# A hybrid decoder layer on one core: three rules and seven DMA issuers changed in a kernel that plans its own instruction order

## The chip, the cores and the metric

The kernel runs on one core of one Trainium2 chip. TensorE (PE), VectorE (DVE), ScalarE (ACT), GpSimd (POOL) and SyncE (SP) each work through their own queue in order; they meet through semaphores, and transfers run beside them. The metric is the device time of one launch in microseconds: the median of three runs before the change is 491.67 us (490.88 to 494.11).

## The reference

One layer on x of 256 tokens by 1024 channels, in float32. A conditioning vector c gives nine vectors of shift, scale and gate. Three sub-layers follow, each normalised first and added to the stream through its gate:

```python
mod = silu(c) @ w_ada + b_ada                       # 1024 x 9216, split in nine
n = modulate(rmsnorm(h, g_ffn1), sh1, sc1)
h = h + 0.5 * gt1 * swiglu(n, w1_gate, w1_up, w1_down)        # 1024 -> 2816 -> 1024
n = modulate(rmsnorm(h, g_mix), sh2, sc2)
h = h + gt2 * hybrid_mixer(n, w_in, w_pool, pool_scale, w_out)
n = modulate(rmsnorm(h, g_ffn2), sh3, sc3)
h = h + 0.5 * gt3 * swiglu(n, w2_gate, w2_up, w2_down)
return rmsnorm(h, g_final)
```

The mixer makes u, q, k, v with one projection. Four groups of 128 channels of u go through trailing means over 2, 4, 8 and 16 tokens (minus the token itself), a 128x128 map and a per-channel scale. Eight heads of 64 do causal attention with distance penalties over three sets of strided keys. Both halves are concatenated and projected by w_out.

## The kernel before

**Tiling and number format.** The 256 tokens are two tiles of 128 (t = 0 and 1). Every large product keeps float32 accuracy by three passes: an operand is split into a rounded copy `hi` and the remainder `lo`, and PE adds hi*hi, lo*hi and hi*lo in PSUM (`gemm`, lines 628 to 630; the same in lines 669, 699 and 1010). Weights come in 1 MB pieces named `raw` (SP issues them, line 515). ACT casts half a piece to `hi` (line 531), DVE subtracts to get `lo` (line 532). The conditioning product runs on DVE alone: line 520 reduces a piece of w_ada against silu(c) into columns of `mod`.

**Stages.** First feed-forward (PE tiles `ld`, `gu`, down projection into `accf`), then the mixer (`zp` gives u, q, k, v as `z`; `sc` scores, `p` probabilities, `pt` their transposes, `pts` the copies of those, `yt` the head outputs; `po` the pooled means, `pl` their copy, `pw` the map), then w_out into `accm`, then the second feed-forward (`le`, `gu`, `accf`). Between stages `norm_rows` (lines 565 to 585) works per token tile: the gate row tile `gt` times the accumulator, add to `h`, sum of squares half on ACT (line 575) and half on DVE (line 578), one addition (line 576) and one power (line 581) on GpSimd, scaled rows `xsb` or `xsc`, which PE transposes into `xtb` or `xtc` (line 558).

**The mixer's outputs.** They are split as well: `y[t]` is a pair of tiles, `nhy` (rounded) and `nly` (remainder), one pair for each token tile. Heads: `split` in lines 550 and 551, called from `heads_out` for t = 0, then t = 1, both out of the one PSUM tile `yt`. Pool groups: lines 959 and 960, for t = 0, then t = 1, out of the one PSUM tile `pw`.

**Gate rows.** `gate_rows` turns eight columns of `mod` into a row on all partitions: PE transposes (`gp`, line 617), ACT copies to `gs` (line 619), a transfer writes it to HBM (`gd`, line 621), and another, which waits for that, reads it back to 128 partitions (`gt`, line 623). It is called three times, for the gates of the three sub-layers.

**Mixer constants.** `bias` (two halves, lines 898 and 965), `band_all` (line 966), `wp_all` (line 967) and the final gain `gfb` (line 1042) are loads of 256 to 544 KB. In this kernel ACT issues all of these and the gate rows.

**The order.** `settle` records all instructions and `arrange` plans them five times over with a table of costs (`Item.cost`); the best of the five becomes the order of ACT, DVE and POOL and of PE, and is enforced. Three numbers of the plan matter here. A transfer is taken to have landed `LATE` ns after its modelled end. For PSUM tiles an instruction is put after the latest earlier user of the same tile on the same engine. Among ready instructions the one that is due first goes, looking `SOON` ns ahead. None of these costs is a measurement of this text; they only decide who stands behind whom.

Of the kernel before, what the change touches and what calls it, by code (L numbers as in the profile page):

```python
# [10 lines left out]
F32 = mybir.dt.float32  # L11
F32R = mybir.dt.float32r
AF = mybir.ActivationFunctionType
ALU = mybir.AluOpType

P = 128
S = 256
NT = S // P
D = 1024
# [159 lines left out]
STAGES = ("_ffn1_", "_mix_", "_ffn2_")  # L179
LANES = 8  # L180
SOON = 1400
LATE = 1000
PASSES = 5


# [88 lines left out]
def arrange(items, tiles, before):  # L274

    num = range(len(items))
    preds, history, uses, latest = [], {}, {}, {}
    for n in num:
        x, found = items[n], set(before.get(n, ()))
        for mine, accesses in ((False, x.reads), (True, x.writes)):  # L280
            for name, rows, mask in accesses:
                for k, wrote, r, m in history.get(name, ()):
                    if (wrote or mine) and r & rows and m & mask:
                        found.add(k)
        for mine, accesses in ((False, x.reads), (True, x.writes)):
            for name, rows, mask in accesses:
                kept = history.setdefault(name, [])
                if mine:
                    kept[:] = [e for e in kept if e[2] | rows != rows or e[3] | mask != mask]
                kept.append((n, mine, rows, mask))  # L290
                if n not in uses.setdefault(name, []):
                    uses[name].append(n)
                found.add(uses[name][0])
                if "_psp_" in tiles[name].tag or "_accp_" in tiles[name].tag:
                    found.add(latest.get((name, x.eng), n))
                    latest[name, x.eng] = n
        found.discard(n)
        preds.append(sorted(found))
    succs = [[] for _ in num]
# [15 lines left out]
    for _ in range(PASSES):  # L315
# [25 lines left out]
        while sum(map(len, order.values())) < len(items):  # L341
            pick = None
            for e in SIGNAL:
# [5 lines left out]
                if e == "PE":  # L349
                    n = min((n for n in at if at[n] <= t0 + 40), key=lambda n: items[n].prio)  # L350
                else:
                    now = sorted((n for n in at if at[n] <= t0 + 20), key=lambda n: due[n])
                    n = now[0]
                    if expect:
# [10 lines left out]
                        if h and u in at and near[u] + items[u].taken - due[n] - shift < h - 50:  # L365
                            n = u
# [80 lines left out]
def block_kernel(ctx, tc, w, vec, x, c, gf, wpool, bandd, biasd, out):  # L447
# [101 lines left out]
    def split(hi_ap, lo_ap, src):  # L549
        nc.scalar.copy(hi_ap, src)  # L550
        nc.vector.tensor_tensor(lo_ap, src, hi_ap.bitcast(F32), ALU.subtract)  # L551
# [61 lines left out]
    def gate_rows(gtm, factor):  # L613

        assert all(gtm * KD + j in done_mod for j in range(KD))
        pt = psp.tile([KD, P], F32, name=f"gp{gtm}", tag="ps")
        nc.tensor.transpose(pt, mod[:, ts(gtm, KD)], ident)
        sb = work.tile([KD, P], F32, name=f"gs{gtm}", tag="gs", bufs=1)
        nc.scalar.activation(sb, pt, AF.Copy, scale=factor)
        d = dram.tile([KD, P], F32, name=f"gd{gtm}", tag=f"gd{gtm}")  # L620
        nc.scalar.dma_start(d, sb)
        g = work.tile([P, D], F32, name=f"gt{gtm}", tag="gt", bufs=1)
        nc.scalar.dma_start(g, d.rearrange("(o a) b -> o (a b)", o=1).to_broadcast([P, D]))
        return g


# [268 lines left out]
    bias = [xp.tile([P, 4 * S], F32, name="bias0")]  # L895
    band_all = xp.tile([P, 4, 2 * P + 16], F32, name="band_all")
    wp_all = xp.tile([P, 4 * P], F32, name="wp_all")
    nc.scalar.dma_start(bias[0], biasd[:, 0:4 * S])

    def scores(hp):  # L900

# [24 lines left out]
    def heads_out(hp, v, y):  # L926
        pts = []
        for hd in (2 * hp, 2 * hp + 1):
            pt = psp.tile([P, 3, P], F32, name=f"pt{hd}", tag="ps")
            for i in range(3):  # L930
                nc.tensor.transpose(pt[:, i, :], probs[hd][:, ts(i, P)], ident)
            sb = xp.tile([P, 384], F32, name=f"pts{hd}", tag="pts", bufs=2)
            with urgent():
                nc.scalar.copy(sb, pt.rearrange("p a b -> p (a b)"))
            pts.append(sb)
        ps = psp.tile([P, S], F32, name=f"yt{hp}", tag="ps")
        for t, cs, qs in ((0, slice(0, S), slice(0, S)), (1, slice(P, S), slice(S, 384))):
            for e in range(2):
                mm(ps[e * DH:e * DH + DH, cs], v[t][:, ts(2 * hp + e, DH)], pts[e][:, qs], start=t == 0, stop=t == 1)
        with urgent():  # L940
            for t in range(NT):
                split(y[t][0][:, 4 + hp, :], y[t][1][:, 4 + hp, :], ps[:, ts(t, P)])

    def pool_group(g, u, y):
        bands, wp = band_all[:, g], wp_all[:, ts(g, P)]
# [9 lines left out]
        with urgent():  # L955
            sc = vecs[:, PS + g:PS + g + 1]
            for t in range(NT):
                yh, yl = y[t]
                nc.scalar.activation(yh[:, g, :], p2[:, ts(t, P)], AF.Copy, scale=sc)
                nc.vector.scalar_tensor_tensor(yl[:, g, :], p2[:, ts(t, P)], sc, yh[:, g, :].bitcast(F32),  # L960
                                               ALU.mult, ALU.subtract)

    after = finish1(1)
    bias.append(work.tile([P, 4 * S], F32, name="bias1", tag="gt", bufs=1))
    nc.scalar.dma_start(bias[1], biasd[:, 4 * S:8 * S])
    nc.scalar.dma_start(band_all, bandd)
    nc.scalar.dma_start(wp_all, wpool)
    QS = -DH ** -0.5
    y = [new_n(f"y{t}") for t in range(NT)]
    z = {}  # L970
# [68 lines left out]
        lead_step(1, j, n3, (2, 3, 0, 1), lead)  # L1039

    gfb = fp[0].tile([P, D], F32, name="gfb")
    nc.scalar.dma_start(gfb, gf.to_broadcast([P, D]))
    nc.scalar.mul(gfb, gfb, float(D) ** 0.5)

    def finish3(t):
# [69 lines left out]
```

## Time and profile before

| | |
|---|---|
| Median of three runs | 491.67 us (490.88 to 494.11) |
| The profiled execution | 492.43 us, span 490.7 us, mean granted PE clock 0.992 |
| PE busy | 474.2 us (97% of the span) |
| DVE, ACT, POOL busy | 358.2, 263.8, 10.8 us |
| Moved by transfers | 126.06 MB, 257 GB/s on average |

All times of the trace are microseconds from the start of the span. In a timeline row stand start, duration, engine, source line, operation, output<-inputs, shape, how many instructions were merged, and in brackets how long the engine had been idle and what ended that. A row of waits gives who waited for whom: total us, number of times, the longest. PE and ACT are pipelined, so instructions of one engine can overlap in a timeline; steps are then best read from start to start. ACTq is ACT's instruction issue: a transfer that it issues shows there.

### The profile page before, as it was taken

Reading aid. Unit: us, or ns where it says so; the run is one execution under the profiler, and the core shown is the slowest. Engines: PE = TensorE matmul, PEld = TensorE weight load, DVE = VectorE, ACT = ScalarE, POOL = GpSimd, SP = SyncE. Lnnn points to the kernel's source line nnn. Section 1 sums busy time; section 2 is a strip of 40 time slices with the busy share of each in tenths; the row PEclk is TensorE's granted clock in tenths of the full one; section 3 lists DMA queues with packets and bytes.
Section 4 is the critical chain, followed back from the end, with each engine's and each line's share of the span. In section 5 each row is a group of like instructions: output and inputs, shape, how many; then the busy total and the mean of one; then the engine's idle time right before and its main releaser. Section 6 shows DMA issues by size and latency. Waiting matters only on the chain.

```text
span 490.7 us, 6019 instructions
## 1 busy us (share of the span) xinstructions
PE 474.2 (97%) x2176; PEld 383.1 (78%) x2176; DVE 358.2 (73%) x579; ACT 263.8 (54%) x451; POOL 10.8 (2%) x22
## 2 busy tenths in 40 slices
PE   8999999999999999999997999999999999999993
PEld 5688888888888887777775777888888888888882
DVE  4989999987976856888996788755656765655243
ACT  3776676255444444896773486846543543544121
POOL 1000000000000001100000011000000000000000
PEclk9999999999999999999999999999999999999998
DMA  8999995998878882889758687475367758540002
GB/s 304 396 400 359 377 373 201 393 373 342 347 282 313 284 330 75 326 309 372 260 214 317 226 286 255 170 289 217 119 240 261 279 194 321 188 155 28 17 1 86
DMA packets 19232, 126.06 MB, mean 257 GB/s; under 512 B 2281, under 2 KB 3073, under 8 KB 4866
## 3 DMA queue, kind: packets, MB, share of 16 engines
q1 hardware_dynamic: 17568, 121.25, 65.1%
q10 hardware_dynamic: 1634, 4.43, 2.5%
q8 instruction: 17, 0.28, 0.2%
q14 instruction: 13, 0.11, 0.1%
HBM read 124.61 MB, written 1.06 MB: 256 GB/s over the span
## 4 chain that ended last, share of the span: by engine, by line
PE 81%; DVE 5%; DMA 4%; ACT 4%; issue 3%; POOL 2%; ACTq 0%; POOLq 0%; DVEq 0%
PE accf L669 20%; PE gu L628 9%; PE gu L630 9%; PE gu L629 9%; PE ld L699 8%; PE le L699 8%; PE accm L1010 3%; DMA raw<-in_w_dram 3%; PE zp L628 2%; PE zp L630 2%; PE zp L629 2%; PE ht L655 2%; ACT hi L531 1%; DVE lo L532 1%; DMA gd<-gs 1%
## 5 line engine op out<-in xcount | busy, mean ns | idle before, releaser
L532 DVE TENSOR_TENSOR lo<-raw,hi 128x1024 fp32r<-128x1024 f32 (+1 forms) x156 | 184.5, 1208 | 43.2 <-ACT hi L531 34.3
L531 ACT CAST hi<-raw 128x1024 fp32r<-128x1024 f32 (+1 forms) x156 | 159.5, 1043 | 91.8 <-DMA raw<-in_w_dram 34.4
L520 DVE CUSTOM_DVE_ANT_0 raw<-raw,cb,vecs 128x1024 f32<-128x1024 f32 x70 | 88.6, 1280 | 14.7 <-DMA raw<-in_w_dram 14.7
L669 PE MATMUL accf<-hi,hh 128*128 128x512 f32 x176 | 56.6, 395 | 0.2
L669 PE MATMUL accf<-hi,hl 128*128 128x512 f32 x176 | 55.6, 390 | 0.0
L669 PE MATMUL accf<-lo,hh 128*128 128x512 f32 x176 | 55.4, 390 | 0.0
L628 PE MATMUL gu<-hi,nhc 128*128 128x512 f32 x112 | 44.3, 395 | 0.0
L630 PE MATMUL gu<-lo,nhc 128*128 128x512 f32 x112 | 43.7, 390 | 0.0
L629 PE MATMUL gu<-hi,nlc 128*128 128x512 f32 x112 | 43.6, 389 | 0.0
L669 PEld LDWEIGHTS accf<-lo,hh 128*128 128x128 f32 x176 | 33.0, 188 | 7.0
L669 PEld LDWEIGHTS accf<-hi,hl 128*128 128x128 f32 x176 | 32.8, 188 | 7.1 <-DVE hl L551 0.5
L669 PEld LDWEIGHTS accf<-hi,hh 128*128 128x128 f32 x176 | 32.5, 188 | 7.3 <-ACT hh L550 1.1
L646 ACT ACTIVATE sg<-gu 128x256 f32<-128x256 f32 x24 | 9.1, 379 | 48.0 <-PE gu L630 48.0
L628 PE MATMUL gu<-hi,nha 128*128 128x512 f32 x80 | 31.7, 396 | 0.0
L630 PE MATMUL gu<-lo,nha 128*128 128x512 f32 x80 | 31.2, 390 | 0.0
L629 PE MATMUL gu<-hi,nla 128*128 128x512 f32 x80 | 31.1, 389 | 0.0
L649 DVE TENSOR_TENSOR pr<-sg,gu 128x256 f32<-128x256 f32 x24 | 10.0, 417 | 26.3 <-ACT sg L646 26.3
L551 DVE TENSOR_TENSOR hl<-ht,hh 128x256 fp32r<-128x256 f32 x44 | 16.4, 418 | 13.4 <-ACT hh L550 13.4
L628 PE MATMUL zp<-hi,nhb 128*128 128x512 f32 x64 | 26.2, 409 | 0.0
L550 ACT CAST hh<-ht 128x256 fp32r<-128x256 f32 x44 | 14.1, 379 | 22.3 <-PE ht L655 22.3
L630 PE MATMUL zp<-lo,nhb 128*128 128x512 f32 x64 | 25.2, 394 | 0.0
L629 PE MATMUL zp<-hi,nlb 128*128 128x512 f32 x64 | 25.2, 393 | 0.0
(171 smaller groups left out, 718.7 us busy)
## 6 DMA issues: line engine op xcount, KB each, us to landing
raw<-in_w_dram SPq DMA_DIRECT2D x112, 1024.0 KB, 5.7
raw<-in_w_dram SPq DMA_DIRECT2D x4, 512.0 KB, 7.9
gt<-gd ACTq DMA_DIRECT2D x3, 512.0 KB, 3.7
h<-in_x_dram SPq DMA_DIRECT2D x2, 512.0 KB, 5.4
bias<-in_bias_dram ACTq DMA_DIRECT2D x2, 512.0 KB, 3.9
out_dram<-o SPq DMA_DIRECT2D x4, 160.0 KB, 2.2
band_all<-in_band_dram ACTq DMA_DIRECT2D x1, 544.0 KB
gfb<-in_gf_dram ACTq DMA_DIRECT2D x1, 512.0 KB, 3.4
```

Source lines behind the costliest of these rows:

```text
L520: nc.vector.tensor_tensor_reduce(r, r, cb, 1.0, vecs[:, m:m + 1], ALU.mult, ALU.add, mod[:, m:m + 1])
L531: nc.scalar.copy(hi[:, o:o + n], src)
L532: nc.vector.tensor_tensor(lo[:, o:o + n], src, hi[:, o:o + n].bitcast(F32), ALU.subtract)
L550: nc.scalar.copy(hi_ap, src)
L551: nc.vector.tensor_tensor(lo_ap, src, hi_ap.bitcast(F32), ALU.subtract)
L628: mm(ps, nh[:, k, :], whi, start=first, stop=False)
L629: mm(ps, nl[:, k, :], whi, start=False, stop=False)
L630: mm(ps, nh[:, k, :], wlo, start=False, stop=last)
L649: nc.vector.tensor_tensor(pr, sg, ps[:, 256:512], ALU.mult)
L669: mm(accs[b], a[:, k, :], cols(ww, 2 * k + b), start=st, stop=sp)
L699: mm(banks[ci][t], n[t][a][:, j, :], cols(ww, lead_set(f, j).index(ci)), start=j == 0 and p == 0, stop=last and p == 2)
L1010: mm(acc2[t][b], a[:, k, :], cols(ww, 2 * kk + b), start=st, stop=sp)
```

## The change

Seven things change, in three groups.

The plan: `LATE` goes from 1000 to 2600, and the rule for PSUM tiles loses the engine, so that an instruction stands after the latest earlier user of the same tile on any engine ("turns" of a bank).

The issuers: the two transfers of `gate_rows`, both halves of `bias`, `band_all`, `wp_all` and `gfb` are issued by GpSimd in place of ACT.

The mixer's outputs: in `heads_out` and `pool_group` the rounded copies of both token tiles come first on ACT, and then both subtractions on DVE.

```diff
--- before.py
+++ after.py
@@ -179,7 +179,7 @@
 STAGES = ("_ffn1_", "_mix_", "_ffn2_")
 LANES = 8
 SOON = 1400
-LATE = 1000
+LATE = 2600
 PASSES = 5
 
 
@@ -292,8 +292,8 @@
                     uses[name].append(n)
                 found.add(uses[name][0])
                 if "_psp_" in tiles[name].tag or "_accp_" in tiles[name].tag:
-                    found.add(latest.get((name, x.eng), n))
-                    latest[name, x.eng] = n
+                    found.add(latest.get(name, n))
+                    latest[name] = n
         found.discard(n)
         preds.append(sorted(found))
     succs = [[] for _ in num]
@@ -618,9 +618,9 @@
         sb = work.tile([KD, P], F32, name=f"gs{gtm}", tag="gs", bufs=1)
         nc.scalar.activation(sb, pt, AF.Copy, scale=factor)
         d = dram.tile([KD, P], F32, name=f"gd{gtm}", tag=f"gd{gtm}")
-        nc.scalar.dma_start(d, sb)
+        nc.gpsimd.dma_start(d, sb)
         g = work.tile([P, D], F32, name=f"gt{gtm}", tag="gt", bufs=1)
-        nc.scalar.dma_start(g, d.rearrange("(o a) b -> o (a b)", o=1).to_broadcast([P, D]))
+        nc.gpsimd.dma_start(g, d.rearrange("(o a) b -> o (a b)", o=1).to_broadcast([P, D]))
         return g
 
 
@@ -895,7 +895,7 @@
     bias = [xp.tile([P, 4 * S], F32, name="bias0")]
     band_all = xp.tile([P, 4, 2 * P + 16], F32, name="band_all")
     wp_all = xp.tile([P, 4 * P], F32, name="wp_all")
-    nc.scalar.dma_start(bias[0], biasd[:, 0:4 * S])
+    nc.gpsimd.dma_start(bias[0], biasd[:, 0:4 * S])
 
     def scores(hp):
 
@@ -939,7 +939,10 @@
                 mm(ps[e * DH:e * DH + DH, cs], v[t][:, ts(2 * hp + e, DH)], pts[e][:, qs], start=t == 0, stop=t == 1)
         with urgent():
             for t in range(NT):
-                split(y[t][0][:, 4 + hp, :], y[t][1][:, 4 + hp, :], ps[:, ts(t, P)])
+                nc.scalar.copy(y[t][0][:, 4 + hp, :], ps[:, ts(t, P)])
+            for t in range(NT):
+                nc.vector.tensor_tensor(y[t][1][:, 4 + hp, :], ps[:, ts(t, P)], y[t][0][:, 4 + hp, :].bitcast(F32),
+                                        ALU.subtract)
 
     def pool_group(g, u, y):
         bands, wp = band_all[:, g], wp_all[:, ts(g, P)]
@@ -955,16 +958,16 @@
         with urgent():
             sc = vecs[:, PS + g:PS + g + 1]
             for t in range(NT):
-                yh, yl = y[t]
-                nc.scalar.activation(yh[:, g, :], p2[:, ts(t, P)], AF.Copy, scale=sc)
-                nc.vector.scalar_tensor_tensor(yl[:, g, :], p2[:, ts(t, P)], sc, yh[:, g, :].bitcast(F32),
+                nc.scalar.activation(y[t][0][:, g, :], p2[:, ts(t, P)], AF.Copy, scale=sc)
+            for t in range(NT):
+                nc.vector.scalar_tensor_tensor(y[t][1][:, g, :], p2[:, ts(t, P)], sc, y[t][0][:, g, :].bitcast(F32),
                                                ALU.mult, ALU.subtract)
 
     after = finish1(1)
     bias.append(work.tile([P, 4 * S], F32, name="bias1", tag="gt", bufs=1))
-    nc.scalar.dma_start(bias[1], biasd[:, 4 * S:8 * S])
-    nc.scalar.dma_start(band_all, bandd)
-    nc.scalar.dma_start(wp_all, wpool)
+    nc.gpsimd.dma_start(bias[1], biasd[:, 4 * S:8 * S])
+    nc.gpsimd.dma_start(band_all, bandd)
+    nc.gpsimd.dma_start(wp_all, wpool)
     QS = -DH ** -0.5
     y = [new_n(f"y{t}") for t in range(NT)]
     z = {}
@@ -1039,7 +1042,7 @@
         lead_step(1, j, n3, (2, 3, 0, 1), lead)
 
     gfb = fp[0].tile([P, D], F32, name="gfb")
-    nc.scalar.dma_start(gfb, gf.to_broadcast([P, D]))
+    nc.gpsimd.dma_start(gfb, gf.to_broadcast([P, D]))
     nc.scalar.mul(gfb, gfb, float(D) ** 0.5)
 
     def finish3(t):
```

No computation, no weight transfer and no tile changes. The order moves at many places by a few rows; two of them, and what GpSimd gets, are these.

ACT at the end of the mixer's projection, before: `hi` are casts of weights, `nhy` of 1874 and 1876 the rounded outputs of token tiles 0 and 1, `gs`, `gd`, `gt` the second gate row, `z_2445` the copy of u for t = 1, `pl` and `pw` the pool groups.

```order
L550 CAST nhy_1874<-yt_2413 128x128
L550 CAST nhy_1876<-yt_2413 128x128
L531 CAST hi_1_2324<-raw_2318 128x1024
L619 ACTIVATE gs_2433<-gp_2431 8x128
L621 DMA gd_2435<-gs_2433 8x128
L889 ACTIVATE z_2445<-zp_2363 128x512
L952 COPY pl_2451<-po_2447 128x256
L623 DMA gt_2437<-gd_2435 128x1024
L959 ACTIVATE nhy_1874<-pw_2453,vecs 128x128
L959 ACTIVATE nhy_1876<-pw_2453,vecs 128x128
L952 COPY pl_2463<-po_2459 128x256
```

The same place after the change (source lines from 941 on are up to three higher).

```order
L942 CAST nhy_1874<-yt_2413 128x128
L942 CAST nhy_1876<-yt_2413 128x128
L531 CAST hi_0_2320<-raw_2318 128x1024
L619 ACTIVATE gs_2433<-gp_2431 8x128
L889 ACTIVATE z_2445<-zp_2363 128x512
L531 CAST hi_1_2324<-raw_2318 128x1024
L955 COPY pl_2451<-po_2447 128x256
L961 ACTIVATE nhy_1874<-pw_2453,vecs 128x128
L961 ACTIVATE nhy_1876<-pw_2453,vecs 128x128
L955 COPY pl_2463<-po_2459 128x256
```

Both transfers of the gate row are gone from ACT, and one weight cast moved from ahead of `z` to behind it, ahead of the first `pl`.

GpSimd from the norm after the first feed-forward on, before: `vb` and `rb` are the addition and the power of that norm (first t = 0, then t = 1), `vc` and `rc` those after the mixer.

```order
L581 TENSOR_TENSOR rb_1755<-vb_1753,mhalf 128x1
L576 TENSOR_TENSOR vb_1856<-vb_1856,deps 128x1
L581 TENSOR_TENSOR rb_1864<-vb_1862,mhalf 128x1
L576 TENSOR_TENSOR vc_2633<-vc_2633,deps 128x1
L581 TENSOR_TENSOR rc_2641<-vc_2639,mhalf 128x1
```

And after the change.

```order
L581 TENSOR_TENSOR rb_1755<-vb_1753,mhalf 128x1
L898 DMA bias_1849<-in_bias_dram 128x1024
L969 DMA band_all<-in_band_dram 128x1088
L970 DMA wp_all<-in_wpool_dram 128x512
L576 TENSOR_TENSOR vb_1856<-vb_1856,deps 128x1
L968 DMA bias_1870<-in_bias_dram 128x1024
L581 TENSOR_TENSOR rb_1864<-vb_1862,mhalf 128x1
L621 DMA gd_2435<-gs_2433 8x128
L623 DMA gt_2437<-gd_2435 128x1024
L1045 DMA gfb<-in_gf_dram 128x1024
L576 TENSOR_TENSOR vc_2633<-vc_2633,deps 128x1
```

Seven issues now stand between the norm's operations, one of them (the second half of `bias`) between the addition and the power of t = 1.

PE at the last pool group and the last pair of heads, before: `pt` and `yt` belong to the heads, `accm` to w_out.

```order
L954 MATMUL pw_2489<-pl_2487,wp_all 128x256
L931 MATMUL pt_2495<-ident,p_2373 128x128 x3
L931 MATMUL pt_2501<-ident,p_2384 128x128 x3
L1010 MATMUL accm_2520<-lo_0_2102,nhy_1874 128x512
L1010 MATMUL accm_2521<-lo_0_2102,nhy_1874 128x512
L939 MATMUL yt_2507<-pts_2499,z_2181 64x256
```

And after the change.

```order
L1013 MATMUL accm_2520<-lo_0_2102,nhy_1874 128x512
L957 MATMUL pw_2489<-pl_2487,wp_all 128x256
L931 MATMUL pt_2495<-ident,p_2373 128x128 x3
L931 MATMUL pt_2501<-ident,p_2384 128x128 x3
L1013 MATMUL accm_2521<-lo_0_2102,nhy_1874 128x512
L1013 MATMUL accm_2520<-hi_1_2105,nhy_1874 128x512
L1013 MATMUL accm_2521<-hi_1_2105,nhy_1874 128x512
L939 MATMUL yt_2507<-pts_2499,z_2181 64x256
```

Two matmuls of w_out that stood behind `yt` now stand ahead of it.

## The prediction

> **What bounds the kernel now.** I read the page's first part first, then the list of what TensorE waited for, then the timelines around the longest waits.
>
> ```profile
> span 490.7 us, 6019 instructions
> PE 474.2 (97%) x2176; PEld 383.1 (78%) x2176; DVE 358.2 (73%) x579; ACT 263.8 (54%) x451; POOL 10.8 (2%) x22
> PE pw L954 <- ACT pl L952: 2.4, 1, 2.4
> PE xtb L558 <- ACT xsb L583: 1.5, 1, 1.5
> PE po L948 <- ACT z L889: 0.8, 1, 0.8
> ```
>
> PE is busy for 474.2 of 490.7 us, so the sum is made where PE stands. The change touches no PE work; it can only shorten or lengthen PE's waits. Two of the three waits shown lie within one stretch, the pool groups at the end of the mixer; `xtb` is in the norm before it. PE's own timeline there:
>
> ```profile
> 259.48 0.39 PE L630 MATMUL zp<-lo,nhb 128*128 128x512 f32 x1
> 261.87 0.49 PE L948 MATMUL po<-band_all,z 128*128 128x128 f32 x2 [0.84 <-ACT z L889]
> 263.11 0.59 PE L954 MATMUL pw<-pl,wp_all 128*128 128x256 f32 x2
> 267.51 1.03 PE L954 MATMUL pw<-pl,wp_all 128*128 128x256 f32 x2 [2.44 <-ACT pl L952]
> 274.88 1.09 PE L939 MATMUL yt<-pts,z 128*64 128x256 f32 x8
> 275.90 0.73 PE L1010 MATMUL accm<-hi,nhy 128*128 128x512 f32 x2
> 276.47 0.62 PE L1010 MATMUL accm<-hi,nly 128*128 128x512 f32 x2
> 276.93 0.63 PE L1010 MATMUL accm<-lo,nhy 128*128 128x512 f32 x2
> ```
>
> From 275.90 on PE runs `accm` without a wait; before that, 16 us hold the four pool groups, the last heads and a few `accm`. The reason stands in ACT's timeline.
>
> ```profile
> 259.47 0.27 ACT L550 CAST nhy<-yt 128x128 fp32r<-128x128 f32 x1 [1.31 <-DVE nly L551]
> 259.63 1.05 ACT L531 CAST hi<-raw 128x1024 fp32r<-128x1024 f32 x1
> 260.58 0.26 ACT L619 ACTIVATE gs<-gp 8x128 f32<-8x128 f32 x1
> 260.87 0.30 ACTq L621 DMA_DIRECT2D gd<-gs  x1
> 261.21 0.60 ACT L889 ACTIVATE z<-zp 128x512 f32<-128x512 f32 x1 [0.38 <-ACT gs L619]
> 262.52 0.37 ACT L952 COPY pl<-po 128x256 f32<-128x256 f32 x1 [0.71 <-PE po L949]
> 265.64 0.36 ACTq L623 DMA_DIRECT2D gt<-gd  x1
> 266.05 0.37 ACT L959 ACTIVATE nhy<-pw,vecs 128x128 fp32r<-128x128 f32 x1 [3.15 <-DMA gd<-gs]
> 266.83 0.37 ACT L959 ACTIVATE nhy<-pw,vecs 128x128 fp32r<-128x128 f32 x1 [0.42 <-DVE nly L960]
> 267.10 0.36 ACT L952 COPY pl<-po 128x256 f32<-128x256 f32 x1
> 269.73 0.37 ACT L952 COPY pl<-po 128x256 f32<-128x256 f32 x1
> 272.72 0.36 ACT L952 COPY pl<-po 128x256 f32<-128x256 f32 x1
> ```
>
> ACT issues `gd`, copies `z` and the first `pl`, and then stands at the issue of `gt`, which needs `gd` in HBM: 260.87 to 265.64, 4.77 us. `nhy` of the first pool group, the next `pl` and so PE's `pw` at 267.51 queue behind it. Besides, each second `nhy` (t = 1) is held by the subtraction of t = 0: 0.42 us per pool group, 1.31 at the heads. The granted clock (third value from the end of a row of windows; behind it the share of the transfer engines and GB/s) adds a cost:
>
> ```profile
> 208.00:210.00 2.00, 0.77 (x7) 0.77 (x8) 1.56 (x4) 1.28 (x3) 0.42 (x1) 1.00 0.95 364
> 266.00:268.00 2.00, 0.48 (x2) 0.40 (x3) 1.12 (x3) 1.00 (x3) 0.00 (x0) 0.94 0.99 397
> 268.00:270.00 2.00, 2.00 (x9) 1.87 (x8) 1.36 (x4) 1.00 (x3) 0.00 (x0) 0.50 0.99 416
> 270.00:272.00 2.00, 2.00 (x11) 1.70 (x9) 1.32 (x3) 0.44 (x2) 0.00 (x0) 0.71 0.89 369
> 274.00:276.00 2.00, 2.00 (x16) 1.28 (x14) 1.51 (x3) 1.42 (x5) 0.00 (x0) 1.00 0.74 295
> 276.00:278.00 2.00, 2.00 (x9) 1.66 (x10) 1.74 (x4) 0.50 (x2) 0.00 (x0) 1.00 0.07 25
> ```
>
> Behind the 2.44 us wait the clock is 0.94, 0.50, 0.71 over three windows: 0.85 of 3 windows of 2 us, so 1.7 us of PE work lost. Behind the 1.5 us `xtb` wait (it ends at 209.2) it stays 1.00. [...]
>
> **The change, part by part: ACT's chain.** I walk the stretch on before's clock, each step by a start-to-start time of the rows above.
>
> The last `zp` ends at 259.48 + 0.39 = 259.87. With both copies of the heads ahead of the subtractions the 1.31 us wait goes, ACT does its cast and `gs` earlier, and `z` can start at about 259.95, bound by `zp`, not at 261.21. `po` (line 948) follows `z` by 261.87 − 261.21 = 0.66, but PE is in the `accm` it has in hand until about 260.85: 1.0 us earlier than before. `pl` follows by 0.65: 261.50. (The order puts one `hi` cast between; by 1.05 us, started at 260.5, it ends about when `pl` is due.) `pw` follows `pl` by 263.11 − 262.52 = 0.59: 262.1. `nhy` needs only `pw`'s 0.59 plus about 0.05: 262.75, where it was 266.05. That is 3.3 us, the largest single step.
>
> Now a pool group turns over in 0.59 (`pl` to `pw`) + 0.64 (`pw` to `nhy`) + 2 × 0.27 (two `nhy` to the next `pl`, by 267.10 − 266.83) = 1.77 us; before it took 2.63 and 2.99 (267.10, 269.73, 272.72). So `pl` stands at 263.3, 265.05, 266.85 in place of 267.10, 269.73, 272.72: 5.9 us ahead at the last. `pw` then at 267.45, its `nhy` pair to 268.65, `pts` behind it, `yt` 0.68 after that at 269.3, and `accm` 275.90 − 274.88 = 1.02 later: 270.35. Gain 5.55 us. Two `accm` that stood behind `yt` stand ahead of it now; one takes (276.93 − 276.47) / 2 = 0.23, so 0.45 more: 6.0. Against it: with both subtractions last, DVE frees the bank of `pw` later, on which the next transposes wait; by one 0.42 step, I take 0.5. **Sum: 5.5 us.** From there PE is without a wait up to the norm, so the gain is kept if that norm's inputs come as much earlier.
>
> **The issuers on GpSimd.** Two queues matter: POOL's own, and what waits for the norm's power.
>
> ```profile
> 194.11 1.46 POOL L581 TENSOR_TENSOR rb<-vb,mhalf 128x1 f32<-128x1 f32 x1 [1.84 <-DVE vb L578]
> 205.49 0.59 POOL L576 TENSOR_TENSOR vb<-vb,deps 128x1 f32<-128x1 f32 x1 [9.92 <-ACT resb L575]
> 206.95 1.47 POOL L581 TENSOR_TENSOR rb<-vb,mhalf 128x1 f32<-128x1 f32 x1 [0.87 <-DVE vb L578]
> L771 POOL TENSOR_TENSOR rx<-vx,mhalf 128x1 f32<-128x1 f32 x2 | 1.1, 552 | 6.0 <-DVE vx L769 6.0
> 206.79 1.22 DVE L532 TENSOR_TENSOR lo<-raw,hi 128x1024 fp32r<-128x1024 f32 x1
> gt<-gd ACTq DMA_DIRECT2D x3, 512.0 KB, 3.7
> 282.81 0.69 DVE L570 TENSOR_TENSOR resc<-accm,gt 128x512 f32<-128x512 f32 x1 [0.77 <-PE accm L1010]
> ```
>
> No row shows what an issue costs GpSimd. Its ends: the 0.30 us of an issue on ACT, and the 1.46 us of GpSimd's slowest operation here. I take 1.0, between them. Three issues (`bias` first half, `band_all`, `wp_all`) start behind `rb` at 195.57 and have 9.92 us until `vb`: free up to 3.3 us each. The second half of `bias` stands between `vb` (ends 206.08) and `rb`. There 0.87 us are idle; and `rb` takes 1.46 us while DVE runs `lo`, but the same power takes 0.55 as `rx`, so `rb` could begin as late as 207.9 and still end at 208.42. Up to 1.85 us that issue is free too, so both ends of the price give nothing. If the cover is gone, every us is one of PE's, since PE already waits 1.5 us there. `gd` leaves at 260.6; with 4.77 and 3.7 us of landing and two issues `gt` lies at about 271, and `resc` asks for it at 282.81 − 5.5 = 277.3. The first and third gate rows and `gfb` have more room or as much. ACT saves 0.30 to 0.36 us for each issue, which counts nowhere else, since ACT is busy 54%.
>
> **The rest of the plan.** Weight casts change places on ACT and DVE, `xtb` stands one matmul earlier, `xtc` of t = 1 three later. Each moves a wait by at most 0.7 us, in both directions; I take 0, and ±1 for the range.
>
> **The rivals.** *Held issue:* GpSimd can't issue while DVE runs. For: `rb` beside `lo` takes 1.46 us against 0.55. The issue would then begin behind DVE's `lo` at 208.01, take 1.0, and `rb` 0.55: 209.56 in place of 208.42, 1.15 us late. Time 491.67 − 5.5 + 1.15 = 487.3. Against: nothing says that an issue reads what an operation reads. [...]
>
> *The norm after the mixer isn't earlier:* one reduction of line 520 now stands directly ahead of `resc`, and its piece comes from a queue that is full (share 0.99) until 270 and has just emptied at about 276 (0.74, then 0.07). Landing at 276 to 277 plus 1.3 us for the reduction gives `resc` at 277.3 to 278.3 in place of 277.3: up to 1 us. A late gate row would cost the same way. With the clock's 1.7 us not won back in full, the gain is 2 to 4: 488.7 in the middle.
>
> *Slower:* an issue costs GpSimd X of several us. From X = 3.3 the three issues delay `vb`, and `rb` ends at 195.57 + 0.59 + 0.55 + 4X = 196.71 + 4X, late by 4X − 11.7; PE's wait then passes 2.44 us, so 1.7 us of clock come on top. It eats the 5.5 us from X = 3.9. At 4.5 it is 6.3 + 1.7 − 5.5 = 2.5 us slower: 494.2. Against: it is three times the upper row.
>
> *Nothing arrives:* a new wait elsewhere in the planned order takes it back, within 1 us of 491.67.
>
> **How the numbers follow.** The profiled execution took 492.43 us (span 490.7 and 1.7 around it), 0.76 above the median, within the runs' own spread; so it becomes 486.9, and the median 491.67 − 5.5 = 486.2. About 1% (4.9 us) is what a measurement of this kernel tells from no change, so faster means below 486.75. Forecast (gain 4.0 to 7.0) 0.55; held issue 0.10; norm not earlier 0.14; slower 0.11, of it 0.08 by over 1%; nothing 0.07; more than 7 won 0.03. Three quarters of the forecast and the last case lie over 1%: 0.44 faster; 0.08 slower; 0.48 the same. The range runs from 484.6 (7 won) to 491.0 (0.7 won); outside are slower, half of nothing, and more than 7: 0.18.
>
> **What would show it.** ACT without idle time released by `gd`, four `pl` less than 2 us apart, no 2.4 us wait of `pw`, and clock 1.00 throughout show the chain. GpSimd's issue rows give X, `rb` of t = 1 ending by 208.5 on this clock shows the free issue. I am wrong if PE's wait for `xtb` grows past 2 us, if `resc` waits for `gt` or for a piece of w_ada, or if PE's waits elsewhere grow by more than 1 us in sum.

## The result

The changed kernel takes 489.72 us in the median of eight runs, the kernel before 491.93 us in eight. The first execution of the changed kernel (592.87 us) had a mean granted clock of 0.754 (0.7 to 0.8 in 38 of the 40 slices of its page); the ratio leaves it out, and the profile after is that of a further execution: 488.74 us, span 487.0. The ratio is 0.9944 with a 95% interval of 0.9921 to 0.9967, that is 2.8 us won. A second set (12 and 23 runs) gave 489.20 against 492.60, ratio 0.9935 (0.9917 to 0.9953): 3.2 us. Forecast were 5.5 us: the direction was right, and the forecast gain was about twice what came.

### The profile page after: what moved, and what is told of

Its sections match the earlier page's. It is cut to its first block, busy times and chain, and to the rows that moved or that the text cites. A ratio compares the mean times of both kernels' runs of the same rounds, so it can differ in the third digit from the quotient of the medians.

```text
span 591.1 us, 6038 instructions
## 1 busy us (share of the span) xinstructions
PE 581.1 (98%) x2176; PEld 409.0 (69%) x2176; DVE 360.2 (61%) x579; ACT 265.2 (45%) x451; POOL 18.6 (3%) x33
## 3 DMA queue, kind: packets, MB, share of 16 engines
HBM read 124.61 MB, written 1.06 MB: 213 GB/s over the span
## 4 chain that ended last, share of the span: by engine, by line
PE 95%; issue 1%; DMA 1%; DVE 1%; ACT 0%; SPq 0%; POOLq 0%; DVEq 0%; POOL 0%; ACTq 0%
PE accf L669 24%; PE ld L699 9%; PE gu L629 9%; PE gu L630 9%; PE le L699 9%; PE gu L628 9%; PE accm L1013 5%; PE zp L630 3%; PE zp L629 3%; PE zp L628 3%; PE ht L655 2%; DMA raw<-in_w_dram 1%; PE ld L628 1%; PE sh L628 1%; PE ld L630 1%
## 5 line engine op out<-in xcount | busy, mean ns | idle before, releaser
L669 PE MATMUL accf<-hi,hh 128*128 128x512 f32 x176 | 67.7, 461 | 0.0
L669 PE MATMUL accf<-hi,hl 128*128 128x512 f32 x176 | 66.4, 455 | 0.0
L669 PE MATMUL accf<-lo,hh 128*128 128x512 f32 x176 | 66.2, 458 | 0.0
L628 PE MATMUL gu<-hi,nhc 128*128 128x512 f32 x112 | 52.6, 470 | 0.0
L629 PE MATMUL gu<-hi,nlc 128*128 128x512 f32 x112 | 51.0, 455 | 0.0
L630 PE MATMUL gu<-lo,nhc 128*128 128x512 f32 x112 | 50.8, 454 | 0.0
L630 PE MATMUL gu<-lo,nha 128*128 128x512 f32 x80 | 37.1, 464 | 0.0
L629 PE MATMUL gu<-hi,nla 128*128 128x512 f32 x80 | 36.7, 458 | 0.0
L630 PE MATMUL zp<-lo,nhb 128*128 128x512 f32 x64 | 29.9, 468 | 0.0
L630 PEld LDWEIGHTS gu<-lo,nhc 128*128 128x128 f32 x112 | 22.6, 201 | 9.6
```

The lines of the kernel that those rows point to most:

```text
L628: mm(ps, nh[:, k, :], whi, start=first, stop=False)
L629: mm(ps, nl[:, k, :], whi, start=False, stop=False)
L630: mm(ps, nh[:, k, :], wlo, start=False, stop=last)
L669: mm(accs[b], a[:, k, :], cols(ww, 2 * k + b), start=st, stop=sp)
```

## The profile after

First the span and PE's waits of the changed kernel (total us, number, longest).

```profile
span 487.0 us, 6038 instructions
PE xtc L558 <- ACT xsc L583: 2.9, 2, 1.5
PE xtb L558 <- ACT xsb L583: 2.1, 2, 1.9
PE ld L699 <- ACT nha L682: 0.8, 1, 0.8
```

The waits of `pw` and `po` are gone. In their place the two waits for `xtc` sum to 2.9 us, where they were 1.4 (0.43 and 0.97), and the longest for `xtb` has gone from 1.5 to 1.9. ACT's timeline at the pool groups shows the part that went as forecast.

```profile
259.98 0.60 ACT L889 ACTIVATE z<-zp 128x512 f32<-128x512 f32 x1 [1.12 <-PE zp L630]
261.48 0.38 ACT L955 COPY pl<-po 128x256 f32<-128x256 f32 x1
262.71 0.63 ACT L961 ACTIVATE nhy<-pw,vecs 128x128 fp32r<-128x128 f32 x2 [0.85 <-PE pw L957]
263.33 0.37 ACT L955 COPY pl<-po 128x256 f32<-128x256 f32 x1
265.13 0.38 ACT L955 COPY pl<-po 128x256 f32<-128x256 f32 x1
266.93 0.37 ACT L955 COPY pl<-po 128x256 f32<-128x256 f32 x1
```

No idle time is released by `gd` any more; the four `pl` stand 1.80 to 1.85 us apart. On PE, the rows that mark the way to the end, of the changed kernel:

```profile
209.41 1.09 PE L558 MATMUL xtb<-ident,xsb 128*128 128x128 f32 x8 [1.89 <-ACT xsb L583]
269.57 1.06 PE L939 MATMUL yt<-pts,z 128*64 128x256 f32 x8
270.56 0.72 PE L1013 MATMUL accm<-hi,nly 128*128 128x512 f32 x2
284.50 1.09 PE L558 MATMUL xtc<-ident,xsc 128*128 128x128 f32 x8 [1.39 <-ACT xsc L583]
298.89 1.09 PE L558 MATMUL xtc<-ident,xsc 128*128 128x128 f32 x8 [1.47 <-ACT xsc L583]
478.43 0.39 PE L669 MATMUL accf<-lo,hh 128*128 128x512 f32 x1
```

And those of them that were not yet shown of the kernel before:

```profile
209.23 1.09 PE L558 MATMUL xtb<-ident,xsb 128*128 128x128 f32 x8 [1.50 <-ACT xsb L583]
289.10 1.09 PE L558 MATMUL xtc<-ident,xsc 128*128 128x128 f32 x8 [0.43 <-ACT xsc L583]
302.55 1.09 PE L558 MATMUL xtc<-ident,xsc 128*128 128x128 f32 x8 [0.97 <-ACT xsc L583]
482.76 0.39 PE L669 MATMUL accf<-lo,hh 128*128 128x512 f32 x1
```

Read the lead from row to row. At `yt` it is 274.88 − 269.57 = 5.3 us, and two `accm` (0.45 us) more have been done by then. At the first `xtc` it is 4.6, at the second 3.7 with three `le` of 0.23 us more done, and 4.3 at PE's last matmul. The clock has a part in it: the profile before holds the 1.7 us of half clock behind `pw`, and no window of this profile (4 us each, read up to 368) is below 1.00. So the mixer gave what was forecast, and the norm behind it took 1.5 us back: 0.96 at the first `xtc` and 0.50 at the second. DVE shows why at the first.

```profile
277.27 1.29 DVE L520 CUSTOM_DVE_ANT_0 raw<-raw,cb,vecs 128x1024 f32<-128x1024 f32 x1 [4.38 <-DMA raw<-in_w_dram]
278.48 0.69 DVE L570 TENSOR_TENSOR resc<-accm,gt 128x512 f32<-128x512 f32 x1
```

DVE stands 4.38 us for a piece of w_ada, and `resc`, which opens the norm, is queued behind that reduction. GpSimd's timeline holds the issues:

```profile
195.56 0.60 POOL L898 DMA_DIRECT2D bias<-in_bias_dram  x1
196.15 0.67 POOL L969 DMA_DIRECT2D band_all<-in_band_dram  x1
206.13 0.56 POOL L968 DMA_DIRECT2D bias<-in_bias_dram  x1
207.13 1.47 POOL L581 TENSOR_TENSOR rb<-vb,mhalf 128x1 f32<-128x1 f32 x1 [0.44 <-DVE vb L578]
259.15 0.55 POOL L621 DMA_DIRECT2D gd<-gs  x1 [50.55 <-ACT gs L619]
263.54 0.53 POOL L1045 DMA_DIRECT2D gfb<-in_gf_dram  x1
```

An issue costs GpSimd 0.53 to 0.71 us, and `rb` still waits for DVE and not for the issue ahead of it. But `gfb` leaves at 263.54, where ACT issued it before at 277.78:

```profile
277.78 0.34 ACTq L1042 DMA_DIRECT2D gfb<-in_gf_dram  x1
```

From issue to landing (the last value of a row of transfers) it takes 13.1 us in the changed kernel and 3.4 us in the kernel before:

```profile
gfb<-in_gf_dram POOLq DMA_DIRECT2D x1, 512.0 KB, 13.1
gfb<-in_gf_dram ACTq DMA_DIRECT2D x1, 512.0 KB, 3.4
```

## The experiments

Each run is named by its label. Two comparisons differ in a single instruction's place: e9_gfb_act from the changed kernel, and e13_gate_only from e10_gate_gfb. The kernels were measured in four sets on four chips, each beside the kernel before, whose medians were 492.60 (e1, e6, e7, e8), 493.75 (e4, e9, e10, e11), 492.27 (e2, e5, e12) and 493.00 us (e13). Kernels of different sets are therefore better compared by their ratios than by their medians. All medians:

| Run | Plan's two rules | Outputs | Issued by GpSimd | Median us | Ratio to before (95%) |
|---|---|---|---|---|---|
| e1_after | changed | changed | all seven | 489.20 | 0.9935 (0.9917 to 0.9953) |
| e8_noiss | changed | changed | none | 486.54 | 0.9875 (0.9847 to 0.9902) |
| e13_gate_only | changed | changed | gate rows | 486.78 | 0.9852 (0.9799 to 0.9905) |
| e10_gate_gfb | changed | changed | gate rows, gfb | 488.02 | 0.9898 (0.9878 to 0.9917) |
| e9_gfb_act | changed | changed | all but gfb | 487.56 | 0.9884 (0.9863 to 0.9906) |
| e7_noouts | changed | before | all seven | 488.54 | 0.9911 (0.9882 to 0.9941) |
| e4_plan | changed | before | none | 486.53 | 0.9866 (0.9846 to 0.9886) |
| e11_late | LATE only | before | none | 489.83 | 0.9930 (0.9912 to 0.9948) |
| e12_turns | turns only | before | none | 489.57 | 0.9941 (0.9913 to 0.9969) |
| e5_gate | before | before | gate rows | 489.12 | 0.9927 (0.9903 to 0.9952) |
| e2_issuers | before | before | all seven | 490.46 | 0.9953 (0.9923 to 0.9984) |
| e6_noplan | before | changed | all seven | 493.01 | 1.0010 (0.9993 to 1.0028) |

**One part undone.** First the changed kernel again and three kernels with one part put back.

> The changed kernel again, for a profile at full clock. Theory A (the chain was won, something else was lost): pool groups turn over in about 1.8 us, accm runs without a wait from 5 to 6 us earlier than before's 275.90 (270 to 271), and some 2.7 us of new PE waits stand elsewhere in the trace. Theory B (the chain was only won in part): accm starts at about 273, and no new wait is seen elsewhere. Theory C (clock): waits fall by 5 us in sum, but the granted clock is at half for longer, in other places. Time by all: 489 to 490.

Theory A held at its core (`accm` at 270.56, new waits elsewhere), but only 1.5 us of the lost time are new waits in the norm after the mixer; the rest is told below.

The next cut shows two of the seven transfers; the other five change in the same way.

```diff
-        nc.gpsimd.dma_start(d, sb)
+        nc.scalar.dma_start(d, sb)
...
-    nc.gpsimd.dma_start(gfb, gf.to_broadcast([P, D]))
+    nc.scalar.dma_start(gfb, gf.to_broadcast([P, D]))
```

> The changed kernel with all seven transfers issued by ACT again (plan and outputs as changed). Theory A and B: ACT stands again at the gate row's second issue for 3 to 5 us, PE waits for pl, and the time is 491.5 to 493. Rival (the issuers did nothing, the gain came from plan and outputs): 489 to 490.

486.54 us: both named theories and the rival missed. ACT as issuer is 2.7 us *faster* than GpSimd. Its ACT timeline:

```profile
258.91 0.30 ACTq L621 DMA_DIRECT2D gd<-gs  x1
261.51 0.38 ACT L955 COPY pl<-po 128x256 f32<-128x256 f32 x1
263.36 0.37 ACT L955 COPY pl<-po 128x256 f32<-128x256 f32 x1
263.39 0.36 ACTq L623 DMA_DIRECT2D gt<-gd  x1
```

With the later landing in its model the plan puts the issue of `gt` behind the second `pl`, and by then `gd` is in HBM: it issues at 263.39 without a stand. So the wait that the prediction took away by the issuer is already gone by the plan.

```diff
-            for t in range(NT):
-                nc.scalar.copy(y[t][0][:, 4 + hp, :], ps[:, ts(t, P)])
...
+            for t in range(NT):
+                split(y[t][0][:, 4 + hp, :], y[t][1][:, 4 + hp, :], ps[:, ts(t, P)])
```

> The changed kernel with each token tile's copy and subtraction side by side again (plan and issuers as changed). By the prediction's chain 1.0 us at z and 0.4 us for each pool group come back: 1.5 to 3 us slower than the changed kernel, 491 to 492.5. Rival (those waits are covered once ACT no longer stands): same as the changed kernel, 489 to 490.

488.54 us: the waits did not come back. The rival was right about that, and rather too high in the time; the intervals of this kernel and of the changed one overlap. Under the turns the plan puts other work between the two copies (ACT waits for `nly` only 0.37 and 0.29 us, and PE does not wait for it).

```diff
-LATE = 2600
+LATE = 1000
...
-                    found.add(latest.get(name, n))
-                    latest[name] = n
+                    found.add(latest.get((name, x.eng), n))
+                    latest[name, x.eng] = n
```

> The changed kernel with the plan's two rules as before (LATE 1000, turns per engine). By the prediction the plan is worth nothing: 489 to 490. Theory A with the plan as the loser: the lost 2.7 us come back, 486.5 to 487.5. Rival (the plan gave part of the gain): 490.5 to 492.

493.01 us: no expectation reached that far. Without the rules the other two parts together are worth nothing. The trace shows the copies and the subtractions come apart: ACT has made three copies by 253.0, and DVE, which ran reductions in between, starts three subtractions only at 258.03. PE's waits in this run:

```profile
PE pt L931 <- DVE nly L944: 2.7, 1, 2.7
PE yt L939 <- ACT pts L934: 1.4, 1, 1.4
```

The transposes of a later pair wait 2.7 us for these subtractions; they do not read what those write, but `pt` and `yt` take turns in the four PSUM buffers of one pool (`psp`), so I take it that they wait for such a buffer; no run shows that by itself. Against e2_issuers below, which has the outputs as before and is otherwise the same, the new order of the outputs costs 0.57 of a per cent here (1.0010 against 0.9953; the intervals lie apart).

**Which transfer.** Two kernels take `gfb` and the constants apart.

```diff
-    nc.gpsimd.dma_start(gfb, gf.to_broadcast([P, D]))
+    nc.scalar.dma_start(gfb, gf.to_broadcast([P, D]))
```

> The changed kernel with one transfer, the final gain gfb, issued by ACT again, behind the last heads; every other instruction stays where it was. Theory gfb (issued 7 us earlier, it pushes back the piece of w_ada that stands ahead of resc): that piece lands at about 275.7 and not 277.25, resc of t = 0 starts at 277.1 and not 278.5, PE waits for xtc no more, 1.4 us faster than the changed kernel: 487 to 488. Rival clock (PE's 1.9 us wait at xtb is the loss): as the changed kernel, 489 to 489.5.

487.56 us by this one edit: 1.6 less than the changed kernel by the medians, 2.1 by the spans of the two profiles (484.9 and 487.0), 0.5 of a per cent by the ratios, whose intervals lie apart. ACT and DVE of this run:

```profile
270.79 0.33 ACTq L1045 DMA_DIRECT2D gfb<-in_gf_dram  x1
```

```profile
275.78 1.28 DVE L520 CUSTOM_DVE_ANT_0 raw<-raw,cb,vecs 128x1024 f32<-128x1024 f32 x1 [2.83 <-DMA raw<-in_w_dram]
277.08 0.69 DVE L570 TENSOR_TENSOR resc<-accm,gt 128x512 f32<-128x512 f32 x1
```

`gfb` leaves 7.3 us later, the piece of w_ada lands 1.5 us earlier, `resc` starts 1.4 us earlier, and the wait for the first `xtc` is gone. Theory gfb was right. Of the 2.1 us between the two profiles, 1.45 stand at PE's last matmul (476.98 for 478.43) and 0.6 behind it.

The next cut is against e8_noiss; its three lines for ACT are left out.

```diff
+        nc.gpsimd.dma_start(d, sb)
...
+        nc.gpsimd.dma_start(g, d.rearrange("(o a) b -> o (a b)", o=1).to_broadcast([P, D]))
...
+    nc.gpsimd.dma_start(gfb, gf.to_broadcast([P, D]))
```

> The kernel with ACT as issuer of all (e8_noiss) with only the gate rows and gfb moved to GpSimd; the order of PE and DVE is the same. Theory gfb: the piece lands at 277 again, PE waits 1.4 us for xtc: 488 to 488.5. Rival (the loss comes from the constants that GpSimd issues in the norm before the mixer): 486.5 as e8_noiss.

488.02 us, as theory gfb said; the first `xtc` waits 1.15 us. Its neighbour e13_gate_only, in which ACT issues `gfb` again:

> The changed kernel with the constants and gfb issued by ACT again and only the gate rows by GpSimd; it differs from e10_gate_gfb in the issue of gfb alone. Theory gfb: the piece of w_ada lands at 275.7 again, no PE wait for the first xtc, and since PE's wait for xtb is 0.9 us, all executions at a clock of 0.994 or more: 486 to 486.7. Rival (gate rows on GpSimd cost by themselves): 488 as e10_gate_gfb.

486.78 us, 1.2 less by the medians; the first `xtc` does not wait. The interval of its ratio is wide, since the kernel before ranged from 491.83 to 498.51 us in that set, and overlaps that of e10_gate_gfb; but five of its six executions span 484.8 to 485.1 us, and those of e10_gate_gfb 486.1 to 487.4. DVE's wait for the piece, first of e10_gate_gfb, then of e13_gate_only:

```profile
276.71 1.28 DVE L520 CUSTOM_DVE_ANT_0 raw<-raw,cb,vecs 128x1024 f32<-128x1024 f32 x1 [4.13 <-DMA raw<-in_w_dram]
275.75 1.28 DVE L520 CUSTOM_DVE_ANT_0 raw<-raw,cb,vecs 128x1024 f32<-128x1024 f32 x1 [2.94 <-DMA raw<-in_w_dram]
```

Against e8_noiss (486.54) the gate rows on GpSimd cost nothing that these runs can tell. In both pairs the issuer of `gfb` and the moment of its issue change together (GpSimd at 263.3 to 263.5, ACT at 270.6 to 270.8). No run sends it early from ACT, so whether the early moment alone does it, or the other queue has a part, was not separated.

**The parts alone.** Each on the kernel before.

```diff
-LATE = 1000
+LATE = 2600
...
-                    found.add(latest.get((name, x.eng), n))
-                    latest[name, x.eng] = n
+                    found.add(latest.get(name, n))
+                    latest[name] = n
```

> The kernel before with only the plan's two rules changed. Theory plan (a transfer taken to land later is planned later, so the issue of gt moves behind a second pl and ACT no longer stands): 486.5 to 488. By the prediction the issuers are needed for that: 491 to 492.

486.53 us: the two rules alone, three lines, give 5.6 to 7.6 us (1.14 to 1.54% of 493.75), as much as the best of the others and more than the whole change. The prediction had this kernel at 491 to 492.

> The kernel before with LATE 2600 alone, without the turns across engines. Theory plan, by LATE: the issue of gt stands behind the second pl too, ACT does not stand, and the reduction that waited ahead of resc stands behind it: 487 to 488.5. Rival (the turns are the part that counts): 491 to 492.

> The kernel before with only the turns across engines (LATE stays 1000). The issue of gt stands behind the first nhy but still ahead of the second pl. Theory plan, by LATE: ACT stands there for 1 to 4 us and PE waits for pl: 489.5 to 492. Rival (the turns give the gain): 486.5 to 488.

489.83 and 489.57 us: each rule alone gives about half. The first lies between its two expectations and meets neither; the second is in the range of theory plan, but not for its reason. LATE alone removes ACT's stand, but each second `nhy` still waits 0.42 us. The turns alone remove most of those, and `gt` was no long stand either, against the expectation; ACT and PE of e12_turns:

```profile
262.43 0.37 ACT L959 ACTIVATE nhy<-pw,vecs 128x128 fp32r<-128x128 f32 x1 [0.85 <-PE pw L954]
263.61 0.36 ACTq L623 DMA_DIRECT2D gt<-gd  x1
264.06 0.37 ACT L952 COPY pl<-po 128x256 f32<-128x256 f32 x1 [1.27 <-PE accm L1010]
```

```profile
264.49 0.70 PE L954 MATMUL pw<-pl,wp_all 128*128 128x256 f32 x2 [0.73 <-ACT pl L952]
```

```diff
-        nc.scalar.dma_start(d, sb)
+        nc.gpsimd.dma_start(d, sb)
...
-        nc.scalar.dma_start(g, d.rearrange("(o a) b -> o (a b)", o=1).to_broadcast([P, D]))
+        nc.gpsimd.dma_start(g, d.rearrange("(o a) b -> o (a b)", o=1).to_broadcast([P, D]))
```

> The kernel before with only the gate rows' two transfers issued by GpSimd; gfb, the constants, the plan's rules and the outputs as before. By the prediction's chain ACT no longer stands: the first nhy of the pool groups comes at 262.75 and not 266.05, the half clock behind it goes, and each second nhy still waits 0.42 us: 3.5 to 5 us faster than before. Rival (the issuer matters only together with the plan): within 1 us of before.

489.12 us, 3.2 less than before by its median; the interval (0.7 of a per cent, 0.5 to 1.0) holds 3.5 and not 5. This is the prediction's mechanism for the issuer by itself. ACT in this run:

```profile
262.47 0.37 ACT L952 COPY pl<-po 128x256 f32<-128x256 f32 x1 [0.71 <-PE po L949]
263.70 0.37 ACT L959 ACTIVATE nhy<-pw,vecs 128x128 fp32r<-128x128 f32 x1 [0.85 <-PE pw L954]
264.49 0.37 ACT L959 ACTIVATE nhy<-pw,vecs 128x128 fp32r<-128x128 f32 x1 [0.42 <-DVE nly L960]
```

The 3.15 us stand is gone, and with it the half clock: no window of this profile (4 us each, up to 368) is below 1.00, and none of its ten executions has a mean clock below 0.994. The 0.42 us waits stay. The first `nhy` comes at 263.70 and not at 262.75, for without the new order of the outputs `z` still starts at 261.20.

> The kernel before with all seven transfers issued by GpSimd, plan's rules and outputs as before. By the prediction 3.5 to 5 us faster than before. Theory plan: in this order a weight cast whose piece lands late stands behind the first pl, so ACT stands there in place of the gate row's issue, and gfb comes early as in the changed kernel: 0 to 2 us faster than before.

490.46 us, 1.8 less by the medians, about what theory plan said; the interval (0.2 to 0.8 of a per cent) does not exclude 3.5 us. Here a weight cast stands behind the first `pl` and waits 1.02 us for its piece:

```profile
263.88 1.05 ACT L531 CAST hi<-raw 128x1024 fp32r<-128x1024 f32 x1 [1.02 <-DMA raw<-in_w_dram]
```

The outputs' new order was not tried alone on the kernel before. Without the two rules it costs 0.57 of a per cent (e6_noplan against e2_issuers); with them, and ACT as issuer, it gives nothing (e8_noiss 486.54, e4_plan 486.53).

**The clock.** Executions of the changed kernel fall on two spans: of the twelve of e1_after, seven at 486.9 to 487.6 with a clock of 0.994 or 0.995, five at 488.0 to 489.1 with 0.991 or 0.992. Four more single executions were profiled to catch one of the longer kind.

> The changed kernel, one more look: its executions fall on two values 1.8 us apart at clocks of 0.995 and 0.992. Theory clock: if this one is of the longer kind, one stretch of 2 to 4 us at half clock follows PE's 1.9 us wait for xtb, or one of the waits for xtc, and all else is as in the other profile. Rival: the longer kind shows the same clock and another wait.

> The changed kernel, one more look, for an execution at a clock of 0.992. Theory clock: half clock for some 3 us behind the 1.9 us wait for xtb or one of the waits for xtc; rival: another wait at the same clock.

> As e1c_after: half clock behind the wait for xtb or xtc if the execution is of the longer kind; none if it is of the shorter.

> As e1c_after: half clock behind the wait for xtb or xtc if the execution is of the longer kind; none if it is of the shorter.

e1b_after (487.3, 0.995) and e1d_after (487.2, 0.995) were of the shorter kind and show no halved clock: the `zp` behind `xtb` take 0.39 to 0.48 us each. e1c_after (span 488.8, clock 0.992) and e1e_after (488.7, 0.991) were of the longer; there most of them take 0.60 to 0.63 us, from 210.84 to 214.22 and from 211.08 to 213.21. Windows of e1c_after (the clock is the third value from the end):

```profile
208.00:210.00 2.00, 0.56 (x5) 0.56 (x6) 1.54 (x3) 1.21 (x2) 0.63 (x1) 1.00 0.53 211
210.00:212.00 2.00, 2.00 (x10) 1.71 (x9) 1.74 (x3) 1.86 (x6) 0.00 (x0) 0.72 0.51 66
212.00:214.00 2.00, 2.00 (x6) 1.53 (x5) 1.64 (x4) 2.00 (x7) 0.00 (x0) 0.50 0.88 365
214.00:216.00 2.00, 2.00 (x11) 1.63 (x11) 1.53 (x2) 2.00 (x7) 0.00 (x0) 0.93 0.23 94
```

The 1.9 us wait for `xtb` ends at 209.44, in a window at 1.00; the three windows behind it, at 0.72, 0.50 and 0.93, cost (0.28 + 0.50 + 0.07) × 2 = 1.7 us; `yt` stands at 271.19 in this run, 1.6 later than in the shorter kind. The order is the same, and PE's waits at `xtb` and `xtc` agree within 0.2 us. The same wait of 1.9 us is in e9_gfb_act (spans 484.9 to 487.0, three of six at 486.4 or more with clocks of 0.992 to 0.994; the profiled one, at 0.996, has no window below 1.00 up to 368). It is not in e13_gate_only, where PE's list reads

```profile
PE xtb L558 <- ACT xsb L583: 1.0, 2, 0.9
PE zp L629 <- DVE nlb L603: 0.5, 1, 0.5
```

and none of the 17 executions of e13_gate_only, e8_noiss and e10_gate_gfb is below 0.994. PE starts the second `xtb` at the same time (209.34 there, 209.41 in the changed kernel), but it has waited in two pieces of 0.5 and 0.9 us. On DVE a single row stands elsewhere: with the constants on ACT the plan puts a subtraction of `nlb` behind the second half of `resb` and not ahead of it.

## Why the prediction was off in size

**What bounds the kernel: right.** The loss between the last `zp` and the steady `accm` was there and could be taken away; `accm` starts at 270.56, and the walk said 270.35.

**ACT's chain: right step by step.** `pw` at 262.08 (walk: 262.1), `nhy` at 262.71 (262.75), the last `pl` at 266.93 (266.85), `yt` at 269.57 (269.3). The 0.5 us held back for the bank of `pw` was twice what was lost (5.3 + 0.45 of 6.0). What the walk did not see is that the plan alone brings this about: it credited the issuers and the outputs, and e8_noiss has the same chain with ACT as issuer, e4_plan with the outputs as before too (last `pl` at 267.01, `yt` at 269.43). The row for it was in the trace, `gd` at 260.87 and `gt` at 265.64. With ACT as issuer too the stand ended in e8_noiss and e4_plan, where the issue of `gt` stands behind the second `pl`, 4.5 and 4.6 us behind that of `gd`.

**The issuers: the bounds of the price held, the room did not.** 0.53 to 0.71 us for an issue lie within the ends of 0.30 and 1.46 (1.0 was taken), and no norm waits for one. The step that failed reads "The first and third gate rows and `gfb` have more room or as much". It asked when `gfb` is needed, and not what its 512 KB push back. Sent at 263.54 and not at 277.78, it is under way until 276.63, beside the piece of w_ada ahead of `resc`; that piece lands at 277.25 in the changed kernel and 275.76 with `gfb` back on ACT at 270.79. One of the prediction's own signs of being wrong came true with it: `resc` waits for a piece of w_ada. The rival "the norm after the mixer isn't earlier" named the place and took 1 us; it measured 1.2 us at `resc` (278.48 for 277.3) and 0.96 at PE. Its gain of 2 to 4 us is what came, though it had a chance of 0.14; that `gfb` delays the piece was not in it. The rival's other term, that the 1.7 us of clock might stay in part, no run shows at this place: behind `pw` no window of the changed kernel's profile or of e5_gate is below 1.00.

**The rest of the plan: not zero.** Two waits that were taken at 0 in sum were mis-sized. `xtb` one matmul earlier (0.23) and a vb chain 0.18 us later make a wait of 1.9 us from 1.5. That was put at "at most 0.7 us, in both directions"; in fact the longer wait was followed by half clock in two of five profiles. The prediction had seen this behind 2.44 us and not behind 1.5, and did not price a wait between them. And the second `xtc`, three `le` later, was to wait less than 0.97 us and waits 1.47. By the rows, DVE waits for a cast and then runs two `lo` directly ahead of its `resc` (first row, the changed kernel), where one stood without a wait (second row, the kernel before):

```profile
289.64 2.36 DVE L532 TENSOR_TENSOR lo<-raw,hi 128x1024 fp32r<-128x1024 f32 x2 [0.85 <-ACT hi L531]
294.44 1.22 DVE L532 TENSOR_TENSOR lo<-raw,hi 128x1024 fp32r<-128x1024 f32 x1
```

The same wait of 1.45 to 1.47 us is in e8_noiss, e9_gfb_act, e10_gate_gfb and e13_gate_only, so it belongs to the order and not to an issuer. That the two `lo` make it is read from the rows and was not tried by a run.

**The sum again:** 5.3 at `yt`, plus 0.45 for two `accm` done, minus 0.96 and 0.50 at the two `xtc`, is 4.3, which is the lead at PE's last matmul (the leads at the two `xtc` agree with this sum to 0.2 us). The span gains 3.7, so the tail behind that matmul is 0.6 us longer (487.0 − 478.43 = 8.57 against 490.7 − 482.76 = 7.94). It is so in all five profiles of the changed kernel and in no other kernel by as much (e7_noouts, with the same issuers, has 485.4 − 477.37 = 8.0). ACT issues its last output 4.14 us behind that matmul in both kernels, so the difference lies in the landing of the outputs: those that SP issues take 2.8 us in the median, 2.2 before and 2.4 in e9_gfb_act. Why they do stays open. Ten of 23 executions of the changed kernel (three of seven in the first set, five of twelve, two of four) are of the longer kind and pay 1.6 us, 0.7 in the mean, which leaves 3.0; the two sets measured 2.8 and 3.2. Two of the ten were profiled and show the half clock; of the others only the span and the mean clock are known. On the side of the kernel before nothing is taken off, since the profiled span of 490.7 lies near the median of 490.9 of its 72 executions beside these runs.

**The clock as a certainty: wrong.** The walk counted the half clock behind `pw` as lost in every execution of the kernel before. Of those 72 executions, 29 show a mean clock of 0.994 or more (median span 490.1) and 43 less (491.5). If each of the 43 has this half clock, which only the one profile shows, it comes in about six of ten (e5_gate, without the stand ahead of that wait, has none below 0.994 in ten), and a walk that takes it as certain overstates what its removal gives by some 0.6 us (four tenths of 1.4, an estimate).

**The rivals.** Held issue fell: the three issues from 195.56 on take 0.54 to 0.67 us each while DVE subtracts weights for most of that time (`lo` from 193.95 to 196.30 and from 196.62 to 198.97). The slow issue fell too: the longest of GpSimd's issues takes 0.71 us. On the clock the prediction's reading, that 1.5 us leaves it and 2.44 us does not, came from a single execution; half clock follows a gap of 1.9 us in two profiles (e1c_after, e1e_after).

## What to carry to other kernels

Price a transfer that moves to an idle engine by what it displaces as well as by when it is needed: here an early issue of something that nobody waited for was a landing 1.5 us later of something that somebody did. Where an engine stands at an issue, look for whatever can move the issue behind more work on the same engine before changing the engine; here three lines of a plan were worth more than the whole change. And one long wait of TensorE can be worse than two shorter ones after which the same row starts at the same time: here half clock cost 1.7 us behind one wait of 1.9 us in e1c_after, and none of the 17 executions of e13_gate_only, e8_noiss and e10_gate_gfb, with waits of 0.5 and 0.9 us in its place, has a mean clock below 0.994.

## What was not expected of the hardware

A TensorE wait of 1.9 us was followed by a halved clock in two of the five profiles of the changed kernel (1.7 us lost over three windows in e1c_after, `zp` of 0.63 us in place of 0.39 in e1e_after), and span and mean clock put ten of its 23 executions with these two. One of 2.4 us was in the profile of the kernel before (0.94, 0.50, 0.71); one of 2.7 us in the profile of e6_noplan was not (1.00 in every window up to 368), and no profiled wait of 1.5 us was. So the length of a wait does not settle it. Nor is 1.5 us shown to be safe: two of the twelve executions of e12_turns, whose longest wait is 1.5 us where it was profiled, have a mean clock of 0.992 and 0.993. The issue of a load of 512 or 544 KB costs GpSimd 0.53 to 0.67 us where ACT spends 0.33 to 0.45. And `gfb`, 3.4 us from issue to landing when ACT sent it at 277.78 (the transfer engines were 0.07 busy in the 2 us before), took 13.1 us when GpSimd sent it at 263.54, with shares of 0.79 to 1.06 from 264 to 276; the piece of w_ada beside it landed 1.5 us later than with `gfb` on ACT at 270.79.
